# Gate and up projections: the activations' high and low parts in two runs instead of interleaved

## The chip, the cores and the metric

The kernel runs on one core of one Trainium2 chip. The metric is the device time of one execution in microseconds (us), the median of several runs; lower is better.

## What is computed

The reference is one decoder block over 272 positions (16 meta tokens and 256 of the sequence) with model width 2048: a norm, a wide input projection, RWKV-7 time mixing and a forgetting attention side by side, a gated merge, an output projection, and then the feed-forward part, which is where the change lies:

```python
h = h + merged @ w_o
gate, up = jnp.split(_rms(h, n2) @ w_gu, 2, axis=-1)   # w_gu: 2048 x 11264
return h + (jax.nn.silu(gate) * up) @ w_dn             # w_dn: 5632 x 2048
```

Only the 256 positions of the sequence are returned, so the feed-forward part works on 256 positions.

## The kernel before

**Split products.** Every float32 operand is split into a high part (rounded to TensorE's fp32r format) and a low part (the rest). A product is then high times high, high times low and low times high, added up in PSUM. ScalarE makes the high part of a weight tile (`wh`, line 335) and VectorE its low part (`wl`, line 336), each from one 512 KB load `raw` of 128 partitions by 1024 numbers.

**Gate and up.** The loop at line 1385 runs over 11 groups of 512 columns of `w_gate_up`; each group first does gate (tile names `gt`), then up (`up`). `cm_jobs` (line 450) cuts each into 8 jobs (one load of weights each). A job holds two channel tiles `kt` of the contraction (2 of 16; each is 128 channels on the 128 partitions), and runs over 4 blocks of 128 output columns (`m`), and inside over the two channel tiles: so TensorE's order is even `kt`, odd `kt`, even `kt`, odd `kt`, with a new PSUM bank at each even one. For each `m` and `kt`, `mm2` (line 437) issues two matmuls, a **pair**: one of 512 columns (line 441: the weights' high part against the high 256 and the low 256 positions of that channel tile, an access of two pieces of 256), and one of 256 columns (line 443: the weights' low part against the high 256 positions). For the last channel tile (`kt` = 15) the 256-column matmul comes first (line 440). That makes 11 x 2 x 8 x 8 = 1408 pairs, 2816 matmuls. Each matmul has a weight load of its own (128 columns, PEld in the profile), which runs beside the matmul ahead of it.

**The activations.** `hts` holds both parts. In before it is a tile of 16 channel tiles x 2 parts x 272 numbers (L = NMETA + T = 16 + 256; the first 16 of each 272 are not used here). So within a partition the high part of a channel tile begins 64 bytes into its 1088, the low part 1088 bytes further on, and the next channel tile 2176 bytes on. As 2176 is 8 x 256 + 128, the start of an even channel tile and that of an odd one differ by 128 modulo 256, and all even ones are alike modulo 256. The weights' places (`PLACE`, line 59, used at lines 331 to 334) are the same modulo 256 for all four buffers of `wh`, and for all four of `wl`.

**Who writes and reuses hts.** Each of four column groups of the output projection (`wo`, line 1337) ends with transposes, a scaling and a `split` into `hts` (line 1353). After gate and up, the tile's memory is used again for `sst` (line 1414), sums of pairs for the products of the down projection (`dn` and `dnp`).

**Other stages named below.** `zg` (the gate projections of the first half, line 1233) uses `mm2` and `PLACE` as gate and up do, on `xhl`, which is laid out like the old `hts`. `br` (line 1283) uses `mm3` (three matmuls of 256 columns) and the places `APART`, by which the weights of an odd channel tile lie 128 bytes further modulo 256 than those of an even one, as its activations do. `dn` (lines 1460 to 1462) uses three matmuls of 512 columns, with the weights as the moving operand; those alternate by 128 bytes modulo 256 as well.

**What sets the order.** TensorE's instructions stand in the order in which they are written; other engines are scheduled around them. Waits follow from tiles, not from parts of tiles.

Of the kernel before, what the change touches and what calls it, by code (L numbers as in the profile page):

```python
# [10 lines left out]
F32R = mybir.dt.float32r  # L11
# [7 lines left out]
P = 128  # L19
D = 2048  # L20
NMETA = 16

T = 256
L = NMETA + T
# [3 lines left out]
DFF = 5632  # L28
# [6 lines left out]
KT = D // P  # L35
# [23 lines left out]
PLACE = (0, 16, 24)  # L59
APART = (1, 32, 32)  # L60
PLACE_T = (8, 16)

LANES = 108
BETWEEN = 2
# [52 lines left out]
def hybrid_block(ctx, tc, A, out, dbg=None):  # L117
# [18 lines left out]
    def aux_ps(name):  # L136
        return psa.tile([P, 512], F32, tag="aux", name=name)
# [88 lines left out]
    def vc(name, i=0):  # L226
        c = COLS[name] + i
        return vcol[:, c:c + 1]
# [132 lines left out]
    def kblock(ap):  # L361
        return ap.rearrange("(k p) c -> p k c", p=P)

    def mm3(ps, wh, wl, ah, al, first, last):
        nc.tensor.matmul(ps, wh, ah, start=first, stop=False)  # L365
        nc.tensor.matmul(ps, wh, al, start=False, stop=False)  # L366
        nc.tensor.matmul(ps, wl, ah, start=False, stop=last)  # L367
# [29 lines left out]
    def slot(ns):  # L397


        clock[0] += ns  # L400
        if clock[0] < clock[1]:
            return
        due = sorted((st for st in streams if st[0] <= clock[0]), key=lambda st: st[0])
        group = []
        for st in due:
            if st[2] and st[2][0] == "fox":
                mate = [c for c in streams if c[2] and c[2][0] == "chain" and st[2][1] + c[2][1] <= 8 - PSM]
                if mate and mate[0][0] > clock[0] and clock[0] < st[0] + HOLD and mate[0][0] < st[0] + HOLD:
                    continue
                group = [c for c in mate if c[0] <= clock[0]] + [st]  # L410
            else:
                group = [st]
                if st[2]:
                    group += [c for c in due if c[2] and c[2][0] == "fox" and st[2][1] + c[2][1] <= 8 - PSM][:1]
            break
        if group:
            clock[2] = 0.0
            for st in group:
                stage(st)
            clock[1] = clock[0] + max(GAP, MIX * clock[2])  # L420

    def finish_job():
        if pending:
            pending.pop()()

    def run(jobs):
        for load, mul in jobs:
            w = load()
            finish_job()
            pending.append(lambda w=w, mul=mul: mul(w))  # L430
# [6 lines left out]
    def mm2(ps, wh, wl, act, first, last):  # L437

        if last:
            nc.tensor.matmul(ps[:, :T], wl, act[:, 0, :], start=False, stop=False)  # L440
        nc.tensor.matmul(ps.rearrange("p (a t) -> p a t", a=2), wh, act, start=first, stop=last)  # L441
        if not last:
            nc.tensor.matmul(ps[:, :T], wl, act[:, 0, :], start=False, stop=False)  # L443

    def halves(dst, ps):

        nc.scalar.activation(dst, ps[:, :T], AF.Copy)
        nc.vector.tensor_tensor(dst, dst, ps[:, T:], op=ALU.add)

    def cm_jobs(wap, nk, act, n0, n, post, alloc=main_ps, name="cm", two=True, lay=PLACE):  # L450


        box = []
        cols = wap.shape[1]
        nm, kb = cols // P, 1024 // cols

        def mk(q):
            def load():
                return wload([(P, 0, [kb, cols], [((ALL,), kblock(wap[q * kb * P:(q + 1) * kb * P, :]))])], 1024,
                             lay=lay)  # L460

            def mul(w):
                (wh, wl), = w
                if q == 0:
                    box.extend(alloc(f"{name}_{m}") for m in range(nm))
                for m in range(nm):
                    ms = slice(m * P, (m + 1) * P)
                    for k in range(kb):
                        kt = q * kb + k
                        a = act[:, kt, :, n0:n0 + n]  # L470
                        if n == T and two:
                            mm2(box[m], wh[:, k % 2, k // 2, ms], wl[:, k % 2, k // 2, ms], a, kt == 0, kt == nk - 1)
                        else:
                            mm3(box[m][:, :n], wh[:, k % 2, k // 2, ms], wl[:, k % 2, k // 2, ms], a[:, 0], a[:, 1],
                                kt == 0, kt == nk - 1)
                        slot(3 * n / 2.4)
                if q == nk // kb - 1:
                    post(box)
            return load, mul
        return [mk(q) for q in range(nk // kb)]  # L480
# [28 lines left out]
    def split(hi, lo_, src):  # L509
        nc.scalar.activation(hi, src, AF.Copy)  # L510
        nc.vector.tensor_tensor(lo_, src, hi.bitcast(F32), op=ALU.subtract)
# [169 lines left out]
    def rwkv_jobs(g):  # L681
# [14 lines left out]
        for nm, off, full in (("k", 1024, True), ("v", 2048, True), ("r", 0, False)):  # L696
            n0, n = (0, L) if full else (14, T + 2)
            jobs += cm_jobs(w_in[:, off + c0:off + c0 + 256], KT, xhl, n0, n, post(nm, off, full), name=f"{nm}{g}", lay=APART)
# [512 lines left out]
    gt = None  # L1211
# [36 lines left out]
    gt = gt_pool.__enter__()  # L1248
# [52 lines left out]
    hp = hp_pool.__enter__()  # L1301
    hh = hp.tile([P, 2, D], F32, tag="hh", name="hh")

    hts = hp.tile([P, KT, 2, L], F32R, tag="hts", name="hts")
    ss2 = hp.tile([P, 2, 4], F32, tag="ss2", name="ss2")
    rs2 = hp.tile([P, 2], F32, tag="rs2", name="rs2")
    rsb2 = hp.tile([P, T], F32, tag="rsb2", name="rsb2")

    def tm_jobs(wap, nk, ah, al, post, name, lay=PLACE_T):

# [26 lines left out]
    for j in range(4):  # L1337
        js = slice(j * 512, (j + 1) * 512)
        nc.sync.dma_start(hh[:, :, js], x[:, js].rearrange("(t p) c -> p t c", p=P))

        def post(t, ps, j=j, js=js):
            nc.vector.tensor_tensor(hh[:, t, js], ps, hh[:, t, js], op=ALU.add)
            jk = hp.tile([P, 512], F32, tag="jk", name=f"jk{j}{t}", bufs=2)
            nc.scalar.activation(jk, hh[:, t, js], AF.Square, accum_out=ss2[:, t, j:j + 1])
            if t == 0:
                return
            for k in range(4 * j, 4 * j + 4):
                pt = aux_ps(f"hT{k}")[:, :T]
                for t in range(2):
                    nc.tensor.transpose(pt[:, t * P:(t + 1) * P], hh[:, t, k * P:(k + 1) * P], ident)  # L1350
                tmp = hp.tile([P, T], F32, tag="htmp", name=f"htmp{k}", bufs=3)
                nc.vector.tensor_scalar(tmp, pt, vc("n2", k), None, op0=ALU.mult)
                split(hts[:, k, 0, NMETA:], hts[:, k, 1, NMETA:], tmp)
        run(tm_jobs(A["w_o"][0][:, js], KT, mgh, mgl, post, f"wo{j}"))
    finish_job()
    nc.vector.tensor_reduce(rs2, ss2, axis=AX.X, op=ALU.add)
# [27 lines left out]
    wgu = A["w_gate_up"][0]  # L1384
    for j in range(DFF // 512):
        gs = [hp.tile([P, T], F32, tag="ga", name=f"ga{j}{m}", bufs=8) for m in range(4)]

        def post_gate(pss, gs=gs):
            for g, ps in zip(gs, pss):
                halves(g, ps)  # L1390
                nc.vector.tensor_tensor(g, g, rsb2, op=ALU.mult)
                nc.scalar.activation(g, g, AF.Silu)

        def post_up(pss, gs=gs, j=j):
            for m, (g, ps) in enumerate(zip(gs, pss)):
                ub = hp.tile([P, T], F32, tag="ub", name=f"ub{j}{m}", bufs=2)
                halves(ub, ps)
                nc.vector.tensor_tensor(ub, ub, rsb2, op=ALU.mult)
                nc.vector.tensor_tensor(ub, ub, g, op=ALU.mult)
                split(ach[:, 4 * j + m, :], acl[:, 4 * j + m, :], ub)  # L1400
        run(cm_jobs(wgu[:, j * 512:(j + 1) * 512], KT, hts, NMETA, T, post_gate, name=f"gt{j}"))
        run(cm_jobs(wgu[:, DFF + j * 512:DFF + (j + 1) * 512], KT, hts, NMETA, T, post_up, alloc=aux_ps, name=f"up{j}"))

# [5 lines left out]
    fast = FAST  # L1411
    slow = [i for i in range(NF // 2) if i not in fast]
    acp_h, acp_l = (t.rearrange("p (i k) (t c) -> p i k t c", k=2, t=2) for t in (ach, acl))
    sst = hp.tile([P, KT, 2, L], F32R, tag="hts", name="sst").rearrange("p k a t -> p (k a t)")
    sst = sst[:, :len(fast) * 6 * P].rearrange("p (i s a c) -> p i s a c", i=len(fast), s=3, a=2)

    def sums_of_pairs():
# [47 lines left out]
    def split_tiles():  # L1465
        return [wp.tile([P, WCOLS], F32R, tag=t, name=t, bufs=WB).rearrange("p (r c) -> p r c", c=L)[:, :, s:s + T]
                for t, s in zip(("wh", "wl"), PLACE_T)]

    def slow_jobs(i, cg, cs, end):
        def mk(x_):  # L1470
            def load():
                j = 2 * cg + x_
                return wload([(P, 0, [2, 512], [((ALL,), kblock(wdn[i * 256:(i + 1) * 256, j * 512:(j + 1) * 512]))])],
                             1024, lay=(None, *PLACE_T))

# [160 lines left out]
```

## Time and profile before

| | |
|---|---|
| median of 3 runs | 1522.12 us (1520.21, 1522.12, 1522.53) |
| profiled execution, first to last instruction (its span) | 1517.7 us |
| median less span | 4.4 us |
| gate and up, from the first matmul to the last | 788.8 to 1278.1 us |
| TensorE busy share of the span | 99% |

The profile gives no time of the profiled execution other than its span. A row of the trace names the line, the engine, the operation, and the tiles (out<-in). A matmul's shown duration runs past the start of the next one, since matmuls are pipelined: the step from one start to the next is what adds up to time.

### The profile page before, as it was taken

The numbers are of one execution on the slowest core, as the hardware profiler recorded it, in microseconds if no ns is written. First come the engines' busy times: TensorE is split into PE (matmuls) and PEld (weight loads), VectorE is DVE, ScalarE is ACT, GpSimd is POOL, SyncE is SP. The second block draws the span as 40 slices with busy tenths as digits, with TensorE's granted clock in tenths as the row PEclk, the third lists the DMA queues.
The fourth block names the chain that finished last, engine by engine and source line by source line (L and its number), as shares of the span: only waits on it lengthen the run. The fifth ranks groups of instructions, "written<-read, shape, count | busy, mean of one in ns | idle before, by whom it ended". The sixth has DMA issues, their size and how long they took to land.

```text
span 1517.7 us, 26174 instructions
## 1 busy us (share of the span) xinstructions
PE 1509.9 (99%) x10071; PEld 1339.5 (88%) x10071; DVE 1112.0 (73%) x2009; ACT 808.3 (53%) x1230; POOL 99.3 (7%) x182
## 2 busy tenths in 40 slices
PE   9999999999999999999999999999999999999998
PEld 9999999999989888998888888888888888887887
DVE  7888699689789857875665666566566658879776
ACT  7664565475465545644554555454455545554543
POOL 2112202202202000000000000000000000000000
PEclk9999999999999999999999999999999999999999
DMA  8557456646645757777566666666666666566664
GB/s 271 166 166 212 119 156 185 170 122 173 188 127 149 223 152 214 234 231 240 181 179 192 189 187 193 191 186 192 190 187 191 193 186 182 178 211 201 213 206 138
DMA packets 210365, 283.32 MB, mean 187 GB/s; under 512 B 24320, under 2 KB 129296, under 8 KB 210240
## 3 DMA queue, kind: packets, MB, share of 16 engines
q1 hardware_dynamic: 205344, 277.25, 61.9%
q10 hardware_dynamic: 4896, 4.40, 0.9%
q8 instruction: 79, 1.29, 0.3%
q14 instruction: 46, 0.38, 0.1%
HBM read 274.36 MB, written 7.24 MB: 186 GB/s over the span
## 4 chain that ended last, share of the span: by engine, by line
PE 95%; DVE 3%; DMA 1%; issue 1%; ACT 0%; SPq 0%; DVEq 0%; ACTq 0%
PE up L441 11%; PE gt L441 11%; PE zg L441 8%; PE gt L443 5%; PE up L443 5%; PE dn L1461 4%; PE dn L1460 4%; PE dn L1462 4%; PE zg L443 4%; PE f L441 2%; PE br L365 2%; PE br L366 2%; PE br L367 2%; PE f L365 2%; PE wo L1329 2%; PE wo L1331 2%
## 5 line engine op out<-in xcount | busy, mean ns | idle before, releaser
L336 DVE TENSOR_TENSOR wl<-raw,wh 128x1024 fp32r<-128x1024 f32 x460 | 561.9, 1226 | 281.3 <-ACT wh L335 280.6
L335 ACT ACTIVATE wh<-raw 128x1024 fp32r<-128x1024 f32 x460 | 486.5, 1059 | 470.2 <-PE up L441 118.9
L441 PE MATMUL gt<-hts,wh 128*128 128x512 f32 x704 | 242.9, 393 | 0.0
L441 PE MATMUL up<-hts,wh 128*128 128x512 f32 x704 | 242.7, 392 | 0.0
L443 PE MATMUL gt<-hts,wl 128*128 128x256 f32 x660 | 184.8, 280 | 0.0
L443 PE MATMUL up<-hts,wl 128*128 128x256 f32 x660 | 184.6, 280 | 0.0
L441 PE MATMUL zg<-xhl,wh 128*128 128x512 f32 x512 | 181.2, 399 | 0.0
L441 PEld LDWEIGHTS up<-hts,wh 128*128 128x128 f32 x704 | 130.0, 188 | 25.2
L441 PEld LDWEIGHTS gt<-hts,wh 128*128 128x128 f32 x704 | 129.9, 188 | 25.1
L443 PE MATMUL zg<-xhl,wl 128*128 128x256 f32 x480 | 134.3, 280 | 0.0
L443 PEld LDWEIGHTS up<-hts,wl 128*128 128x128 f32 x660 | 125.3, 190 | 1.8
L443 PEld LDWEIGHTS gt<-hts,wl 128*128 128x128 f32 x660 | 125.3, 190 | 1.8
L441 PEld LDWEIGHTS zg<-xhl,wh 128*128 128x128 f32 x512 | 94.3, 188 | 18.7 <-issue 0.7
L1460 PE MATMUL dn<-wh,ach 128*128 128x512 f32 x282 | 110.7, 393 | 0.0
L1461 PE MATMUL dn<-wh,acl 128*128 128x512 f32 x282 | 110.6, 392 | 0.0
L1462 PE MATMUL dn<-wl,ach 128*128 128x512 f32 x282 | 110.5, 393 | 0.0
L443 PEld LDWEIGHTS zg<-xhl,wl 128*128 128x128 f32 x480 | 90.9, 189 | 1.2
L365 PE MATMUL f<-xhl,wh 128*128 128x272 f32 x256 | 75.9, 296 | 0.0
L367 PE MATMUL f<-xhl,wl 128*128 128x272 f32 x256 | 73.6, 288 | 0.0
L366 PE MATMUL f<-xhl,wh 128*128 128x272 f32 x256 | 73.6, 288 | 0.0
L1462 PEld LDWEIGHTS dn<-wl,ach 128*128 128x128 f32 x282 | 52.9, 187 | 12.3 <-DVE wl L336 0.3
L1461 PEld LDWEIGHTS dn<-wh,acl 128*128 128x128 f32 x282 | 52.9, 188 | 12.0
(493 smaller groups left out, 3056.7 us busy)
## 6 DMA issues: line engine op xcount, KB each, us to landing
raw<-in_w_gate_up_dram SPq DMA_DIRECT2D x176, 512.0 KB, 4.3
raw<-in_w_in_dram SPq DMA_DIRECT2D x160, 512.0 KB, 3.9
raw<-in_w_down_dram SPq DMA_DIRECT2D x74, 512.0 KB, 5.0
raw<-in_w_o_dram SPq DMA_DIRECT2D x32, 512.0 KB, 4.3
raw<-in_w_branch_a_dram SPq DMA_DIRECT2D x16, 512.0 KB, 4.6
raw<-in_w_branch_b_dram SPq DMA_DIRECT2D x16, 512.0 KB, 5.0
raw<-in_w_down_dram SPq DMA_DIRECT2D x28, 256.0 KB, 4.6
zgd<-zg ACTq DMA_DIRECT2D x30, 128.0 KB, 3.8
```

The source lines that it names most:

```text
L335: nc.scalar.activation(th, rr, AF.Copy)
L336: nc.vector.tensor_tensor(tl, rr, th.bitcast(F32), op=ALU.subtract)
L365: nc.tensor.matmul(ps, wh, ah, start=first, stop=False)
L366: nc.tensor.matmul(ps, wh, al, start=False, stop=False)
L367: nc.tensor.matmul(ps, wl, ah, start=False, stop=last)
L441: nc.tensor.matmul(ps.rearrange("p (a t) -> p a t", a=2), wh, act, start=first, stop=last)
L443: nc.tensor.matmul(ps[:, :T], wl, act[:, 0, :], start=False, stop=False)
L1329: nc.tensor.matmul(o, ah[:, kt, ts_], hi, start=first, stop=False)
L1331: nc.tensor.matmul(o, ah[:, kt, ts_], lo_, start=False, stop=last)
L1460: nc.tensor.matmul(o, a[0], hi, start=first, stop=False)
L1461: nc.tensor.matmul(o, a[1], hi, start=False, stop=False)
L1462: nc.tensor.matmul(o, a[0], lo_, start=False, stop=last)
```

## The change

`hts` becomes one run of numbers per part: 16 unused numbers, then the high part of all 16 channel tiles one behind the other (16 x 256), then again 16 unused numbers and the low part. `HPART` = 16 x 256 + 16 = 4112 numbers is the distance from a high to its low part (16448 bytes, 64 modulo 256, as 1088 was). A channel tile now follows the one before it at 1024 bytes, so that all 16 start alike modulo 256. The tile shrinks from 34816 to 32896 bytes a partition; its own start is the same byte as before, and what is allocated behind it (`ss2`, `rsb2`, `jk`, `htmp`, `ga`, `ub`, ...) moves down by 1920 bytes. `sst` starts at the same byte. No instruction is added, removed or moved: every engine has the same instructions in the same order, with the same waits; only addresses and one step of an access differ.

```diff
+HPART = KT * T + NMETA
+HTS = 2 * HPART
...
-    hts = hp.tile([P, KT, 2, L], F32R, tag="hts", name="hts")
+    hts = hp.tile([P, HTS], F32R, tag="hts", name="hts")[:, :2 * HPART].rearrange("p (a e) -> p a e", a=2)
+    hts = hts[:, :, NMETA:].rearrange("p a (k t) -> p k a t", t=T)
...
-                split(hts[:, k, 0, NMETA:], hts[:, k, 1, NMETA:], tmp)
+                split(hts[:, k, 0], hts[:, k, 1], tmp)
...
-        run(cm_jobs(wgu[:, j * 512:(j + 1) * 512], KT, hts, NMETA, T, post_gate, name=f"gt{j}"))
-        run(cm_jobs(wgu[:, DFF + j * 512:DFF + (j + 1) * 512], KT, hts, NMETA, T, post_up, alloc=aux_ps, name=f"up{j}"))
+        run(cm_jobs(wgu[:, j * 512:(j + 1) * 512], KT, hts, 0, T, post_gate, name=f"gt{j}"))
+        run(cm_jobs(wgu[:, DFF + j * 512:DFF + (j + 1) * 512], KT, hts, 0, T, post_up, alloc=aux_ps, name=f"up{j}"))
...
-    sst = hp.tile([P, KT, 2, L], F32R, tag="hts", name="sst").rearrange("p k a t -> p (k a t)")
+    sst = hp.tile([P, HTS], F32R, tag="hts", name="sst")
```

## Rows read from the trace of the kernel before

**Rows 1.** The page: busy time, and the granted clock by slices.

```profile
PE 1509.9 (99%) x10071; PEld 1339.5 (88%) x10071; DVE 1112.0 (73%) x2009; ACT 808.3 (53%) x1230; POOL 99.3 (7%) x182
...
PEclk9999999999999999999999999999999999999999
```

**Rows 2.** Busy time by stretches: output projection, gate and up, down projection.

```profile
core 0: us, PE busy (x) PEld busy (x) DVE busy (x) ACT busy (x) POOL busy (x), PEclk, DMA share, GB/s
736.00:789.00 53.00, 53.00 (x239) 42.87 (x238) 31.72 (x40) 24.81 (x35) 0.00 (x0) 1.00 0.61 185
789.00:1278.00 489.00, 489.00 (x2825) 431.45 (x2825) 306.44 (x462) 246.66 (x356) 0.00 (x0) 1.00 0.66 189
1278.00:1517.00 239.00, 235.12 (x1018) 189.96 (x1016) 191.87 (x253) 118.90 (x136) 0.00 (x0) 1.00 0.59 190
```

**Rows 3.** Groups of instructions in 790 to 1277 us; idle time stands last.

```profile
L441 PE MATMUL gt<-hts,wh 128*128 128x512 f32 x702 | 242.2, 393 | 0.0
...
L336 DVE TENSOR_TENSOR wl<-raw,wh 128x1024 fp32r<-128x1024 f32 x176 | 215.5, 1224 | 182.0 <-ACT wh L335 182.0
L335 ACT ACTIVATE wh<-raw 128x1024 fp32r<-128x1024 f32 x175 | 185.8, 1062 | 227.5 <-PE up L441 117.9 <-PE gt L441 105.2 <-PE up L443 2.0
```

**Rows 4.** Tile up, whole trace: durations min/median/max in ns, first and last start.

```profile
L441 PE MATMUL up<-hts,wh x704: 388/393/398, 812.1 to 1278.1; 128*128 128x512 f32 x176
L443 PE MATMUL up<-hts,wl x660: 278/281/283, 812.4 to 1277.9; 128*128 128x256 f32 x165
```

**Rows 5.** TensorE in order of time, five pairs of up: start, duration (us).

```profile
1002.22 0.39 PE L441 MATMUL up<-hts,wh 128*128 128x512 f32 x1
1002.44 0.28 PE L443 MATMUL up<-hts,wl 128*128 128x256 f32 x1
1002.56 0.40 PE L441 MATMUL up<-hts,wh 128*128 128x512 f32 x1
1002.79 0.28 PE L443 MATMUL up<-hts,wl 128*128 128x256 f32 x1
1002.91 0.39 PE L441 MATMUL up<-hts,wh 128*128 128x512 f32 x1
```

**Rows 6.** The same even pair, then the odd one, and the weight loads beside their long matmuls.

```profile
L441 PE MATMUL up<-hts,wh x1: 388/388/388, 1002.2 to 1002.2; 128*128 128x512 f32 x1
L443 PE MATMUL up<-hts,wl x1: 282/282/282, 1002.4 to 1002.4; 128*128 128x256 f32 x1
L441 PE MATMUL up<-hts,wh x1: 397/397/397, 1002.6 to 1002.6; 128*128 128x512 f32 x1
L443 PE MATMUL up<-hts,wl x1: 278/278/278, 1002.8 to 1002.8; 128*128 128x256 f32 x1
...
L443 PEld LDWEIGHTS up<-hts,wl x1: 188/188/188, 1002.2 to 1002.2; 128*128 128x128 f32 x1
...
L443 PEld LDWEIGHTS up<-hts,wl x1: 192/192/192, 1002.6 to 1002.6; 128*128 128x128 f32 x1
```

**Rows 7.** Tile zg, long matmuls of channel tile 13 (odd), then 14 (even).

```profile
L441 PE MATMUL zg<-xhl,wh x1: 392/392/392, 510.4 to 510.4; 128*128 128x512 f32 x1
...
L441 PE MATMUL zg<-xhl,wh x1: 397/397/397, 510.8 to 510.8; 128*128 128x512 f32 x1
```

**Rows 8.** Tile dn, 1292 to 1310 us (one row a line, each third matmul).

```profile
L1461 PE MATMUL dn<-wh,acl x27: 387/388/396, 1291.7 to 1309.6; 128*128 128x512 f32 x27
L1462 PE MATMUL dn<-wl,ach x27: 392/392/393, 1291.9 to 1309.8; 128*128 128x512 f32 x27
```

**Rows 9.** Tile br, TensorE, first and last of six lines with 128 matmuls each.

```profile
L365 PE MATMUL br<-yas,wh x128: 279/280/285, 606.8 to 691.5; 128*128 128x256 f32 x128
...
L367 PE MATMUL br<-ybs,wl x128: 278/281/282, 612.7 to 697.4; 128*128 128x256 f32 x128
```

## The prediction

> **What bounds the kernel now.** I read the page first: TensorE is busy for 99% of the span and its granted clock is full in every slice [rows 1], so time is what TensorE's stream takes, and there is no clock to win back. Then the stretches: gate and up take 489 us, TensorE has no gap in them, VectorE is busy for 306 us of them, ScalarE for 247, the DMA engines for 0.66 [rows 2]. The groups of that stretch say the same from the other side: the matmuls have 0.0 us of idle time before them, while ScalarE's splits of the weights wait 225 us in total for gate and up matmuls to give their tiles back [rows 3]. So the weights come early, TensorE sets the pace, and what the change is worth is the number of matmuls times what each gets shorter or longer. Nothing else can move the end.
>
> **The pace of a pair.** From the first up matmul (812.1 us) to the last (1278.1) are 466.0 us, with the last matmul's own step about 466.2, and they hold 21 groups of 64 pairs [rows 4]: 466.2 / 1344 = 346.9 ns a pair. In order of time the pairs alternate: even channel tile 0.34 us from start to start, odd 0.35 [rows 5]. The durations say it to the ns: even 388 and 282, odd 397 and 278, and the weight load beside the odd long matmul takes 192 ns where that beside the even one takes 188 [rows 6]. A duration is longer than the step to the next start; if by the same amount for all four, it is by (388 + 282 + 397 + 278) / 4 - 346.9 / 2 = 162.8 ns. So an even pair takes 388 + 282 - 325.6 = 344.4 ns and an odd one 349.4. Operation, shapes, engines and weights' residues modulo 256 are the same in both; the activations' start modulo 256 differs by 128. So places in SBUF do show in the time of a matmul here.
>
> **The change, part by part.**
>
> *Nothing is issued more or less, later or earlier.* Instructions, order and waits are unchanged, so there is no term for a new wait, a DMA or a queue.
>
> *The distance of the low part* goes from 1088 to 16448 bytes. Both are 64 modulo 256, the long matmul keeps its access of two pieces of 256 numbers, and I cost it at 0. If only the size of the jump mattered, no row of before prices it; its bounds are those of the whole pair below.
>
> *Tiles behind `hts`* move by 1920 bytes (128 modulo 256). VectorE and ScalarE work on them, with 183 and 242 us of slack in the stretch [rows 2]; these would have to become slower by more than half to be seen. Cost 0. If the slack were gone, TensorE would wait for `wl`, of which there are four buffers.
>
> *The step of 1024 bytes.* This is the term. All channel tiles now start as the even ones did modulo 256, high part and low part, against weights that haven't moved. The price is 1408 pairs times the change of a pair:
> - at the best, each pair has the shorter long matmul and the shorter short one: 388 + 278 - 325.6 = 340.4, or -6.5 ns x 1408 = -9.2 us;
> - all pairs as the even ones: 704 odd pairs lose 5.0 ns, -3.5 us;
> - no change of the mean: 0;
> - all pairs as the odd ones: +2.5 x 1408 = +3.5 us;
> - at the worst, 397 + 282 - 325.6 = 353.4, or +6.5 x 1408 = +9.2 us.
>
> **Why I take 0.** The obvious reading is that the odd pairs' 5 ns are a conflict and go away. Two rows speak against it. In `zg`, which has the same residues, the odd channel tile 13 shows 392 ns and the even tile 14 shows 397 [rows 7]: the long one has changed places, after another run-up (before it stood the reversed order of channel tile 15). So 397 is no property of the even or the odd residue; something is carried from matmul to matmul, and a long one pays for what its predecessors left. And in `dn`, where weights and activations have changed roles and other residues, the matmuls of 512 columns show 387 to 396 ns, yet 26 steps of three take 17.9 us [rows 8]: 17.9 / 78 = 229.5 ns a matmul. In gate and up the mean of the long one is (388 + 397) / 2 - 162.8 = 229.7. Two stages with other places have the same mean and other spreads. I read this as a rate of the matmul with its weight load, around which the starts swing by some ns; places then decide how the time is shared out among neighbours, not how much there is. With a constant residue I expect other, perhaps equal, durations, and about the same 346.9.
>
> The Trainium skill, "SBUF — State Buffer", section "Who interferes with whom", gives TensorE two independent read ports, one for the moving operand and one for weight loads, and says that it waits for nobody. By that rule no address could matter and the change would be worth 0. The 388 against 397 ns, and 188 against 192 for the weight load [rows 6], don't agree with it to the ns, and so I don't rest the sum on it; that the means of two stages agree [rows 4, 8] does go with it.
>
> The sum against the profiled execution: 1517.7 + 0 = 1517.7 us of span. The median of the runs is 4.4 us above that span, so I forecast 1522 us, within 2 us either way if the mean of a pair stays within 1.4 ns.
>
> **The rivals.**
>
> *All pairs as the even ones (faster).* For it: in the steady state of gate and up the even residue is always the shorter pair [rows 5, 6], with the shorter weight load, and the change gives every channel tile just that residue. Against it: rows 7, and that an even matmul so far always came after an odd one; the short 388 may be what follows a long one. Price 704 x 5.0 = 3.5 us: 1518.6 us, and down to 1513 us if the short matmuls fall to 278 as well. It decides for faster once a pair is under 344.8 ns (3.0 us over 1408 pairs).
>
> *A lasting collision (slower).* If the residue at which moving data and weights meet is carried from pair to pair, alternating by 128 bytes may be what breaks it, and a constant one locks every long matmul into the form of 397 ns with a weight load of 192. For it: `br`, where `APART` moves weights and activations together, so that their distance modulo 256 doesn't alternate, takes 697.4 - 606.8 = 90.6 us for 767 steps [rows 9], 118.1 ns, where the matmuls of 256 columns in gate and up take (282 + 278) / 2 - 162.8 = 117.2. By columns that is 0.9 x 3 = 2.7 ns a pair, 3.8 us. Against it: `br` has no matmul of 512 columns and other residues. Price +3.5 us by the odd pairs, +3.8 by `br`: 1525.6 to 1526 us. It decides for slower over 349.0 ns a pair.
>
> **How the numbers follow.** A measurement of this kernel can tell about 0.2% (3 us) from no change. No change of the mean: 0.48, at 1522 us (1520 to 1524). All pairs as the even ones, or better: 0.28, at 1518.6. A lasting collision: 0.24, at 1525.6. So faster 0.28, same 0.48, slower 0.24. The ends at 9.2 us need both matmuls of a pair at their extremes together, which no neighbouring rows show; I leave about 0.1 beyond each end and take 1515.5 to 1527.5.
>
> **What the profile of the changed kernel would show.** Gate and up still without idle time before the matmuls; if there is some, the term is not TensorE's pace and this working is wrong. The alternation in steps of two pairs should be gone or changed, since nothing alternates by channel tile any more; if it is still there, even 388 and odd 397, the residue was never its cause. From the first up matmul to the last 466 us: 463 or less is the faster rival, 469 or more the slower one. Weight loads beside long matmuls at 192 ns throughout show the collision; at 188 throughout with steps of 0.34 us, the even pairs. Output and down projection should stay at 53.0 and 239 us; if they move, the shifted tiles matter, which I cost at nothing.

## The result: slower by 0.17%

| | before | after |
|---|---|---|
| median of 21 runs each | 1520.64 us (1519.54 to 1522.53) | 1523.29 us (1521.76 to 1525.77) |
| profiled execution, span | 1517.7 us | 1520.9 us |
| gate and up, first matmul to last | 788.8 to 1278.1 = 489.3 us | 788.0 to 1279.6 = 491.6 us |

The ratio is 1.0017, with a 95% interval of 1.001 to 1.0023: 1.5 to 3.5 us slower, 2.65 us by the medians. The time lies in the range that I gave, but the case that I took for the likeliest, a pace that stays, did not come about. That 1523.29 us also lies within the 1520 to 1524 us that I gave for that case is luck: I had counted from a median of 1522.12 us over three runs, and over 21 before has 1520.64. One run of before, among those beside the last kernels below, had a granted clock of 0.64 and took 2152.45 us; no figure here includes it.

The page of after first, then the stretches, cut as in [rows 2]; gate and up now last to 1280 us.

```profile
PE 1512.0 (99%) x10071; PEld 1337.6 (88%) x10071; DVE 1111.3 (73%) x2009; ACT 807.7 (53%) x1230; POOL 100.5 (7%) x182
...
PEclk9999999999999999999999999999999999999999
```

```profile
736.00:789.00 53.00, 53.00 (x241) 42.93 (x241) 31.76 (x40) 25.64 (x36) 0.00 (x0) 1.00 0.61 181
789.00:1280.00 491.00, 491.00 (x2821) 430.31 (x2821) 306.39 (x462) 245.83 (x356) 0.00 (x0) 1.00 0.65 189
1280.00:1520.00 240.00, 234.99 (x1015) 189.28 (x1013) 191.50 (x252) 119.12 (x136) 0.00 (x0) 1.00 0.60 189
```

The counts are those of [rows 1], the clock is full, TensorE has no gap in gate and up, and VectorE and ScalarE do the same work in the same time as in [rows 2]. The groups of 790 to 1277 us (as [rows 3]):

```profile
L444 PE MATMUL gt<-hts,wh 128*128 128x512 f32 x701 | 243.0, 394 | 0.0
...
L339 DVE TENSOR_TENSOR wl<-raw,wh 128x1024 fp32r<-128x1024 f32 x175 | 214.2, 1224 | 182.7 <-ACT wh L338 182.7
L338 ACT ACTIVATE wh<-raw 128x1024 fp32r<-128x1024 f32 x174 | 184.5, 1060 | 228.4 <-PE up L444 117.3 <-PE gt L444 106.6 <-PE up L446 2.0
```

There is still 0.0 us before the matmuls, and ScalarE still waits for them, 228 us in place of 227. So in gate and up the same matmuls in the same unbroken stream take longer. Tile `up` over the whole trace, against [rows 4]:

```profile
L444 PE MATMUL up<-hts,wh x704: 390/394/398, 811.4 to 1279.6; 128*128 128x512 f32 x176
L446 PE MATMUL up<-hts,wl x660: 277/279/281, 811.6 to 1279.4; 128*128 128x256 f32 x165
```

From first to last are 468.2 us where before has 466.0. With the last matmul's own 0.23 that is 468.43 / 1344 = **348.5 ns a pair against 346.9**, and 1.6 x 1408 = 2.3 us: the 2.3 us by which gate and up grew, and nearly all of the 2.65. All pace figures below are worked out like this from that row of each kernel (good to 0.1 ns). Of what is left, 0.3 us, nothing can be said: the interval of the medians is 2 us wide.

The two profiled executions differ in two more places. The earlier stages ended 0.8 us sooner in after. Behind gate and up, after took 1.7 us more; most of that is waits of TensorE for the splits of weights in the down projection, before first, then after:

```profile
PE dnp L1460 <- ACT wh L510: 0.5, 1, 0.5
PE dnp L1462 <- DVE wl L511: 0.2, 1, 0.2
```

```profile
PE dnp L1466 <- DVE wl L514: 1.6, 3, 0.8
PE dnp L1464 <- ACT wh L513: 0.5, 1, 0.5
```

(The numbers are us in total, times, and the longest.) These waits come and go without the change: before_w_alt below, on the layout of before, has 2.4 us in place of the 0.2.

In order of time (start, duration in us), five pairs as in [rows 5], and the next that stands eight pairs after the first:

```profile
1002.06 0.40 PE L444 MATMUL up<-hts,wh 128*128 128x512 f32 x1
1002.30 0.28 PE L446 MATMUL up<-hts,wl 128*128 128x256 f32 x1
1002.41 0.39 PE L444 MATMUL up<-hts,wh 128*128 128x512 f32 x1
1002.64 0.28 PE L446 MATMUL up<-hts,wl 128*128 128x256 f32 x1
1002.76 0.40 PE L444 MATMUL up<-hts,wh 128*128 128x512 f32 x1
1003.00 0.28 PE L446 MATMUL up<-hts,wl 128*128 128x256 f32 x1
1003.11 0.39 PE L444 MATMUL up<-hts,wh 128*128 128x512 f32 x1
1003.35 0.28 PE L446 MATMUL up<-hts,wl 128*128 128x256 f32 x1
1003.46 0.39 PE L444 MATMUL up<-hts,wh 128*128 128x512 f32 x1
...
1004.85 0.40 PE L444 MATMUL up<-hts,wh 128*128 128x512 f32 x1
```

The 0.34, 0.35, 0.34, 0.35 of before is gone; these four steps are all 0.35 (rounded), and the pattern repeats after eight pairs (one load of weights) instead of two. The weight loads of the same tile, 1000 to 1003.5 us, and the one among them that takes longest:

```profile
L446 PEld LDWEIGHTS up<-hts,wl x11: 188/189/192, 1000.0 to 1003.5; 128*128 128x128 f32 x11
...
L446 PEld LDWEIGHTS up<-hts,wl x1: 192/192/192, 1001.7 to 1001.7; 128*128 128x128 f32 x1
```

The long form of 192 ns, in [rows 6] beside each odd pair, has become rarer: the median is 189, and over the whole of `up` 77 of 704 loads of `wl` take 192 ns, where in before 308 do.

### The profile page after: what moved, and what is told of

It is laid out like the page before. It is cut to its first block, busy times and chain, and to the rows that moved or that the text cites. A ratio compares the mean times of both kernels' runs of the same rounds, so it can differ in the third digit from the quotient of the medians.

```text
span 1520.9 us, 26174 instructions
## 1 busy us (share of the span) xinstructions
PE 1512.0 (99%) x10071; PEld 1337.6 (88%) x10071; DVE 1111.3 (73%) x2009; ACT 807.7 (53%) x1230; POOL 100.5 (7%) x182
## 4 chain that ended last, share of the span: by engine, by line
PE 94%; DVE 3%; DMA 1%; issue 1%; ACT 0%; SPq 0%; DVEq 0%; ACTq 0%
PE gt L444 11%; PE up L444 11%; PE zg L444 8%; PE gt L446 5%; PE up L446 5%; PE zg L446 4%; PE dn L1465 3%; PE dn L1464 3%; PE dn L1466 3%; PE f L444 2%; PE br L368 2%; PE br L369 2%; PE br L370 2%; PE f L368 2%; PE wo L1333 2%; PE wo L1335 2%
```

## The experiments

The question is which part of the change slows TensorE: the low part lying far away, the tiles behind `hts` having moved, or the channel tiles all starting alike modulo 256; and if it is the last, by what rule. I call three rules R, A and P. **R**: the pace follows from how the moving data lies to the weights that are loaded beside it, and is good as long as that alternates. **A**: each such distance has a price of its own, which adds up over the matmuls. **P**: the operands' own starts modulo 256 count, each by itself.

Distances are given as (long, short): the start of the moving data less the start of the weights loaded beside that matmul, modulo 256, worked out from where the program puts the tiles. Before alternates between (224, 0) and (96, 128) from channel tile to channel tile; after has (224, 0) throughout. `lay` sets the weights' places: whether those of odd channel tiles lie 128 bytes further, and the first number of `wh` and of `wl` (4 bytes each; `PLACE` is (0, 16, 24)). "64 pairs" is the time of one gate or up from its first matmul's start to the next one's, in the trace. The texts put on record ahead of the runs give paces about 0.2 ns lower (346.7 for before, 348.3 for the changed kernel), and two of them give 346.7 for lo_0 as well, where 22.233 us / 64 is 347.4; by 64 pairs all can be compared. One time a kernel, beside one of before on the same chip, except for the last three, which have 15 of before beside them (median 1520.86 us).

| kernel | distances (long, short) | first to last up, us | a pair, ns | 64 pairs, us | time (before beside it), us |
|---|---|---|---|---|---|
| before | (224, 0) / (96, 128) | 466.0 | 346.9 | 22.200 | |
| after | (224, 0) | 468.2 | 348.5 | 22.307 | |
| alt_two_runs | (224, 0) / (96, 128) | 466.0 | 346.9 | 22.200 | 1520.73 (1521.0) |
| const_near | (224, 0) | 468.2 | 348.5 | 22.307 | 1522.04 (1521.0) |
| before_w_alt | (224, 128), weights and activations alternate | 469.8 | 349.7 | 22.387 | 1526.2 (1521.0) |
| after_w_alt | (224, 128) / (96, 0), weights alternate alone | 470.2 | 350.0 | 22.400 | 1525.17 (1521.0) |
| all_odd | (96, 128) | 474.1 | 352.9 | 22.587 | 1528.78 (1520.34) |
| wh_128 | (224, 128) | 465.7 | 346.7 | 22.187 | 1520.05 (1520.34) |
| wl_128 | (96, 0) | 470.2 | 350.0 | 22.400 | 1525.5 (1520.34) |
| lo_0 | (224, 0), low part 64 less | 466.7 | 347.4 | 22.233 | 1520.94 (1520.34) |
| shift_64_all | (224, 0), all 64 further | 468.2 | 348.5 | 22.307 | 1524.92 (1520.29) |
| before_wh_128 | (224, 128) / (96, 0) | 469.1 | 349.2 | 22.347 | 1524.23 (1520.29) |
| one_piece | as lo_0, one access of 512 | 466.7 | 347.4 | 22.233 | 1521.9 (1520.29) |
| wh_128_lo_0 | (224, 128), low part 64 less | 471.9 | 351.3 | 22.480 | 1529.43 (1520.29) |
| wh_64 | (224, 192) | 470.6 | 350.3 | 22.420 | 1524.53 (1520.86) |
| wl_64 | (160, 0) | 470.4 | 350.2 | 22.413 | 1524.14 (1520.86) |
| wh_128_timed | (224, 128) | 465.7 | 346.7 | 22.187 | below |

### Which part of the change

**alt_two_runs** keeps the two runs, a far low part (16704 bytes, 64 modulo 256) and moved tiles (by 1408 bytes, 128 modulo 256 as the 1920 of the change), but puts the odd channel tiles behind the even ones, 128 bytes further modulo 256:

```diff
-HPART = KT * T + NMETA
+HPART = KT * T + NMETA + 64
...
+        o = NMETA + k // 2 * T + k % 2 * (KT // 2 * T + 32)
+        return htile[:, :, o:o + T]
```

> The changed kernel with its two runs kept, but within a run the even channel tiles stand first and the odd ones behind them, 128 bytes further modulo 256; the low part is 16704 bytes (64 modulo 256) behind the high one. So the residues alternate by channel tile as in the kernel before, at the distance of the changed one. Measure: start to start of 64 pairs of gate or up (22.200 us before, 22.307 us changed). Theory R (the alternation of residues modulo 256 sets the pace): 22.20 us, and the alternation of 388 and 397 ns is back. Theory D (the far low part sets it): 22.31 us. Theory S (the shifted tiles behind hts): 22.31 us, as they are shifted here too.

Its tile `up`, and four of its long matmuls among the rest in order of time:

```profile
L453 PE MATMUL up<-hts,wh x704: 388/393/398, 811.3 to 1277.3; 128*128 128x512 f32 x176
```

```profile
1000.03 0.39 PE L453 MATMUL up<-hts,wh 128*128 128x512 f32 x1
...
1000.38 0.40 PE L453 MATMUL up<-hts,wh 128*128 128x512 f32 x1
...
1000.73 0.39 PE L453 MATMUL up<-hts,wh 128*128 128x512 f32 x1
...
1001.07 0.40 PE L453 MATMUL up<-hts,wh 128*128 128x512 f32 x1
```

466.0 us from first to last, as before, with the durations of [rows 4] (388 to 398, median 393) and the alternation of [rows 5] back. So neither the two runs nor the low part's distance beyond its residue nor the moved tiles cost gate and up anything that can be seen.

**const_near** is the opposite: the parts lie near each other again, in groups of two channel tiles, and all tiles start alike modulo 256.

```diff
-HTS = 2 * HPART
+HTS = KT * 2 * L
...
+        o = NMETA + k % 2 * T
+        return htile[:, k // 2, :1056].rearrange("p (a e) -> p a e", a=2)[:, :, o:o + T]
```

> High and low parts interleaved in groups of two channel tiles, low part 2112 bytes behind the high one (64 modulo 256), groups 4352 bytes apart: all channel tiles start alike modulo 256 as in the changed kernel, but the parts lie near each other, and the tile has the size of before, so that nothing behind it is shifted. Theory R: 22.31 us for 64 pairs and the eight-pair pattern of the changed kernel. Theory D and theory S: 22.20 us.

```profile
L453 PE MATMUL up<-hts,wh x704: 390/394/398, 811.6 to 1279.8; 128*128 128x512 f32 x176
```

468.2 us, and after's durations (390, 394, 398). With these two the part is settled: the loss of pace is the constant residue, all of it, with the weights at the places that they have in before.

### By what rule

**before_w_alt and after_w_alt** let the weights of odd channel tiles lie 128 bytes further, on the layout of before and of after: `lay=(1, 16, 24)` for both loops, no other edit.

```diff
-post_gate, name=f"gt{j}"))
+post_gate, name=f"gt{j}", lay=(1, 16, 24)))
...
-post_up, alloc=aux_ps, name=f"up{j}"))
+post_up, alloc=aux_ps, name=f"up{j}", lay=(1, 16, 24)))
```

> The kernel before with hts as it was (residues alternate by 128 bytes), but the weights of the odd channel tiles of gate and up also 128 bytes further modulo 256, so that activations and weights keep their distance modulo 256 and both alternate. Theory R as a relation (what counts is the distance modulo 256 between the moving data and the weights being loaded): 22.31 us as in the changed kernel. Theory R as the activations' own residue (the step from one matmul's moving data to the next one's): 22.20 us as in the kernel before.

> The changed kernel (activations' residue constant) with the weights of the odd channel tiles of gate and up 128 bytes further modulo 256: the distance between moving data and weights alternates by 128 again. Theory R as a relation: 22.20 us and the alternation of 388 and 397 ns, as in the kernel before. Theory R as the activations' own residue: 22.31 us, as in the changed kernel.

```profile
L441 PE MATMUL up<-hts,wh x704: 392/392/400, 811.7 to 1281.5; 128*128 128x512 f32 x176
```

```profile
L444 PE MATMUL up<-hts,wh x704: 392/394/399, 812.2 to 1282.4; 128*128 128x512 f32 x176
```

Both (before_w_alt first) are slower than before and after, 349.7 and 350.0 ns. R as I had put it falls: after_w_alt has the alternation of distances that it asks for, and is the worse for it. Part of that is a mistake of mine: the weights loaded beside a short matmul are those of the next channel tile, so that alternating weights give other distances at the short matmul than alternating activations do, (224, 128) and (96, 0) for after_w_alt in place of before's (224, 0) and (96, 128).

**all_odd, wh_128, wl_128** hold one distance throughout: after's runs 128 bytes further; the weights' high part 128 bytes further; their low part 128 bytes further.

```diff
-HTS = 2 * HPART
+HTS = 2 * HPART + 32
...
-name="hts")[:, :2 * HPART]
+name="hts")[:, 32:]
```

For wh_128 `lay=(0, 48, 24)`, for wl_128 `lay=(0, 16, 56)`.

> The changed kernel with its two runs 128 bytes further on, so that every channel tile starts as the odd ones did before. Call a pair by two distances modulo 256: moving data minus the weights loaded beside it, for the long matmul and for the short one. Before: 224 and 0 for even, 96 and 128 for odd, 346.7 ns on average; changed: 224 and 0 for all, 348.3; this one: 96 and 128 for all. Theory A (each pair has a price by its two distances, and prices add up): 2 x 346.7 - 348.3 = 345.0 ns, 64 pairs in 22.09 us. Theory K (a constant pattern always keeps a collision alive): 348.3 ns or more, 22.31 us or more.

> The changed kernel with the high parts of gate and up weights 128 bytes further on, all of them: distances 224 and 128 for every pair. The kernel of before with alternating weights had the same two distances at alternating places and took 350.0 ns a pair. Theory A: 350.0 ns here too, 22.40 us for 64 pairs, with its pattern of two pairs. If the own places or the steps from one matmul's place to the next matter besides the distances: another number.

> The changed kernel with the low parts of gate and up weights 128 bytes further on: distances 96 and 0 for every pair. The changed kernel with alternating weights mixed 224 and 128 with 96 and 0 and took 350.0 ns on average. Theory A: 2 x 350.0 - 350.0 = 350.0 ns, 22.40 us for 64 pairs. Theory K: 348.3 or more.

all_odd, its tile `up`, and two pairs in order of time:

```profile
L444 PE MATMUL up<-hts,wh x704: 387/395/396, 812.0 to 1286.1; 128*128 128x512 f32 x176
```

```profile
1000.08 0.40 PE L444 MATMUL up<-hts,wh 128*128 128x512 f32 x1
1000.31 0.28 PE L446 MATMUL up<-hts,wl 128*128 128x256 f32 x1
1000.43 0.40 PE L444 MATMUL up<-hts,wh 128*128 128x512 f32 x1
1000.66 0.28 PE L446 MATMUL up<-hts,wl 128*128 128x256 f32 x1
1000.78 0.40 PE L444 MATMUL up<-hts,wh 128*128 128x512 f32 x1
```

Nearly every pair is the same here, at 0.35 us, and first to last takes 474.1 us: the odd residue by itself costs 352.9 ns, the even one (after) 348.5, and alternating between the two (before) 346.9, less than either. wh_128:

```profile
L444 PE MATMUL up<-hts,wh x704: 392/393/399, 811.6 to 1277.3; 128*128 128x512 f32 x176
```

465.7 us: one shift of the weights' high part by 128 bytes gives back what the change lost. A falls with these four: if distances had prices that add up, (224, 0) and (96, 128) would cost together what (224, 128) and (96, 0) cost, but 348.5 + 352.9 = 701.4 ns and 346.7 + 350.0 = 696.7. (The 350.0 of wl_128 is what A had given for it; its 345.0 for all_odd and 350.0 for wh_128 were not met.) Theory K falls with wh_128: a constant pattern needn't be slow. And wh_128 and before_w_alt have (224, 128) at every pair alike, and take 346.7 and 349.7 ns: the distances beside each matmul do not fix the pace.

The edits of `lay` also move what ScalarE and VectorE write. Read from the starts in the traces, that isn't what costs time: in all_odd the pairs that run (for nine tenths of their time or more) during one of ScalarE's splits of weights average 353.3 ns, and so do those that run beside none (a tenth of their time at most); in wh_128 both average 346.7. For VectorE's splits it is 353.3 and 353.4, and 346.6 and 346.7.

**lo_0** takes the 16 unused numbers out between the runs, so that a low part lies 16384 bytes behind its high part, 0 modulo 256 instead of 64. **one_piece** has the same residues, but each low part directly behind its high part, so that the long matmul reads one piece of 512 numbers:

```diff
-HPART = KT * T + NMETA
-HTS = 2 * HPART
+HPART = KT * T
+HTS = 2 * HPART + NMETA
```

```diff
+    hts = hp.tile([P, HTS], F32R, tag="hts", name="hts")[:, NMETA:].rearrange("p (k a t) -> p k a t", a=2, t=T)
```

> The changed kernel with the low run 16384 bytes behind the high one (0 modulo 256) instead of 16448 (64). Distances of the starts stay 224 and 0. If only the data that move while the weights are being loaded count, and these are the high part's, nothing changes: 348.3 ns, 22.31 us. If the low part's place counts too: another number, between 345 and 350 ns by the values seen so far.

> The low part of a channel tile directly behind its high part (1024 bytes), channel tiles 2048 bytes apart, all alike modulo 256: the long matmul reads one piece of 512 numbers in place of two of 256, at the residues of the run with the low part at 0. If the break between two pieces costs anything of its own: under 346.7 ns a pair, up to some 7 ns less (the 16 cycles by which the long matmul is above the short one), 22.2 us down to 21.8. Theory Q: 346.7 ns, 22.23 us, as in that run.

```profile
L444 PE MATMUL up<-hts,wh x704: 389/394/403, 811.9 to 1278.6; 128*128 128x512 f32 x176
```

```profile
L444 PE MATMUL up<-hts,wh x704: 389/394/403, 811.5 to 1278.2; 128*128 128x512 f32 x176
```

Both (lo_0 first): 466.7 us, 347.4 ns, the same durations. So the low part's residue counts too (348.5 to 347.4), and the break between the two pieces of the access costs nothing at these residues.

**shift_64_all** moves activations and both parts of the weights by 64 bytes together (`[:, 16:]` for the activations, `lay=(0, 32, 40)`).

> The changed kernel with the activations' runs and both parts of gate and up weights moved by 64 bytes together: every distance between moving data and weights stays as in the changed kernel, every own place modulo 256 is another. Theory Q (a pair has a floor of 346.7 ns, and what comes on top is decided by distances modulo 256 among the data read, not by the places themselves): 348.3 ns and the same eight-pair pattern, 22.307 us for 64 pairs. Theory P (own places modulo 256 count): another number.

```profile
L444 PE MATMUL up<-hts,wh x704: 390/394/398, 812.3 to 1280.5; 128*128 128x512 f32 x176
```

468.2 us with after's durations. P falls: a shift of all three by 64 bytes changes nothing, so what matters here are places against each other. (Its run was 1524.92 us all told; gate and up account for none of what it has over after.)

**before_wh_128** is before with `lay=(0, 48, 24)`; it alternates between the two distances that after_w_alt alternates between. **wh_128_lo_0** joins two edits that each helped.

> The kernel before with the high parts of gate and up weights 128 bytes further on: distances 224 and 128 for even channel tiles, 96 and 0 for odd ones. The changed kernel with alternating weights had just this sequence of distances between moving data and weights, and took 350.0 ns a pair; only the steps from one matmul's activations to the next one's differ (128 modulo 256 here, 0 there). If the distances between moving data and weights are all that counts: 350.0 ns, 22.40 us. If the steps among the activations count as well: another number, 346.7 or more by theory Q.

> The changed kernel with both of the edits that alone gave 346.7 ns: high parts of the weights 128 bytes further on, and the low run at 0 modulo 256. Theory Q: no pair below the floor, 346.7 ns or more, 22.19 us or more for 64 pairs. If each edit takes 1.7 ns off whatever the other does: 345.0 ns, 22.08 us.

```profile
L441 PE MATMUL up<-hts,wh x704: 388/392/399, 811.9 to 1281.0; 128*128 128x512 f32 x176
```

before_wh_128 took 349.2 ns, after_w_alt 350.0 (22.347 and 22.400 us for 64 pairs): the same distances to the weights, not the same pace, so these distances in their order don't fix it either. What differs between the two is how the activations lie to one another, and how the weights do; which of these has the share wasn't separated. wh_128_lo_0, tile `up`:

```profile
L444 PE MATMUL up<-hts,wh x704: 389/394/408, 813.5 to 1285.4; 128*128 128x512 f32 x176
```

351.3 ns, from two edits that alone gave 346.7 and 347.4: what the edits are worth doesn't add up.

### A version without the loss, and two more places

**wh_128_timed** is wh_128 again, with more runs; **wh_64** (`lay=(0, 32, 24)`) and **wl_64** (`lay=(0, 16, 40)`) look for a pace under 346.7 at distances between.

> The changed kernel with the high parts of gate and up weights 128 bytes further on, timed. By its pace (22.187 us for 64 pairs, against 22.200 before and 22.307 changed) 22 x 0.013 = 0.3 us under the kernel before, which its measurement can't tell from it, and 2.6 us under the changed kernel: ratio to before 0.9995 to 1.000. If the loss of the changed kernel lies elsewhere than in the pace of the pairs: 1.0015 or more.

> The changed kernel with the high parts of gate and up weights 64 bytes further on: distances 224 and 192. Theory Q (a floor): 346.7 ns a pair or more, 22.19 us or more for 64 pairs. Theory V (346.7 is no floor): a value under it.

> The changed kernel with the low parts of gate and up weights 64 bytes further on: distances 160 and 0. Theory Q: 346.7 ns a pair or more, 22.19 us or more. Theory V: a value under it.

wh_128_timed: 1520.14 us median of 11 runs, ratio to before 0.9996, interval 0.9987 to 1.0005; its row repeats to 0.1 us (811.8 to 1277.5). The two runs of memory with the weights 128 bytes further cost what before costs; that they are better can't be told. As its tiles lie where after's do, and only the places of its weights differ, this also bears out that after's loss is the pace. wh_64 and wl_64 took 350.3 and 350.2 ns, slower than after.

## Why the prediction was wrong

**What held.** The bound: in gate and up TensorE's stream has no gap and no waits in either kernel, and what they lost is pace. The jump to the low part and the tiles behind `hts`: 0 in gate and up, as costed, by alt_two_runs, whose jump and shift have other sizes but the same residues, and by wh_128_timed, which has the very 16448 and 1920 bytes and before's time. The alternation of two pairs is gone, as the residue's doing. The output projection takes what it took: its last matmul starts 91.1 us behind its first in both (697.5 to 788.6, 696.6 to 787.7; the 53.0 us of [rows 2] are only the part of it in that window).

"Nothing else can move the end" did not hold to the size of this change: behind the last up matmul the 17 traces take 239.6 to 242.9 us to their ends, for the most part by what TensorE waits in the down projection.

**The step that failed** is "Why I take 0": that a matmul with its weight load has a rate of its own, around which starts swing, and that places only share the time out among neighbours. The places set the rate. Moving nothing but operands, gate and up ran at 346.7, 346.9, 347.4, 348.5, 349.2, 349.7, 350.0, 350.3, 351.3 and 352.9 ns a pair: 1.8% from end to end, 465.7 to 474.1 us in the stretch. What the rate theory had seen may be a floor: of 16 layouts none ran below before's pace by more than 0.2 ns, and two others reach it. If it is one, before stood on it, so that, as far as these layouts tell, the change could only keep the pace or lose; I had no row that said so, and gave 0.28 to a gain.

The 0 entered the sum without a row in which the activations' residue is constant, and it measured +2.3 us (1.6 ns x 1408).

My two rows for it were weaker than I took them to be. [rows 7] did show that 397 ns is no property of a residue, and the sequel bears that out: in lo_0 all pairs have the same residues, and yet (by the starts in the trace) they take 352.9 and 340.5 ns in turn. But "something is carried from matmul to matmul" says only that neighbours count, not that their sum is fixed. [rows 8] compared two stages that both alternate by 128 bytes; equal means there say nothing about a stage that doesn't alternate. The account of the kernel ahead says of `dn` that it alternates; I didn't use it.

**The other numbers of the sum.** The bounds of the term were -9.2 to +9.2 us. The one on the slow side is near what the slowest layout did, 352.9 ns in all_odd against 353.4, but by luck: its matmuls show 395 and 281 ns, for which my sum, with 325.6 ns taken off, gives 350.4. So the amount by which durations run past the next start isn't the same in every layout. The 4.4 us between the span and the median were too large a term as well: in after's 21 runs a time is 1.7 to 2.2 us above its own span, and the rest was the scatter of the runs.

**The faster rival** (all pairs as the even ones) fails as I had argued against it: the short 388 of an even pair in [rows 6] does not stay when no odd pair stands ahead. With the even residue alone the long matmuls take 390 to 398 and the pair 348.5 ns, not 344.4 (by the starts in the trace, before's even pairs take 343.5 ns and its odd ones 350.0). The two states of an alternation aren't to be had one by one: each residue alone is slower than both in turn.

**The slower rival** (a lasting collision) was right in its sign and in that alternating is what kept the pace, for this layout of the weights, and wrong in its form and its price. I had each long matmul at 397 ns beside a weight load of 192, +3.5 us; after has that form only now and then, and +2.3; its 468.2 us from the first up matmul to the last stand between the 466 and the 469 that I had named. And all_odd, the slowest of all, shows what that form is worth as a mark: its weight loads beside the long matmuls stand at 187 to 188 ns from end to end:

```profile
L446 PEld LDWEIGHTS up<-hts,wl x660: 187/188/188, 812.0 to 1285.6; 128*128 128x128 f32 x165
```

So a weight load of 192 ns is not what a slow pace is made of. `br`, from which I had taken +3.8 us, would have been the better neighbour of the two stages that I used, with a distance that doesn't alternate; that it was slow for this reason was not tried.

**The rule cited ahead.** By the Trainium skill, "SBUF — State Buffer", section "Who interferes with whom", moving data and weight loads have independent ports and TensorE waits for nobody. The traces show no wait of a matmul in gate and up, but at the same instructions and the same clock the pace depends on where the operands lie, 346.7 to 352.9 ns; the measurement decides, and the rule can't be used to cost a layout at 0.

**What stays open.** Why a place costs 1.6, 3 or 6 ns a pair. That two reads of TensorE collide is the reading that suggests itself, but no run shows a collision. The modulus of 256 bytes fits the runs: const_near's groups of two channel tiles lie 4352 = 17 x 256 bytes apart and after's tiles 1024, and both take 22.307 us for 64 pairs, while 128 bytes make a difference (before against after). Moves that aren't multiples of 64 bytes weren't tried. The three rules tried (R, A, P) are refuted as single rules. What is shown is that places count relative to each other and in sequence: distance to the weights beside (wh_128, wl_128), residue of the low part (lo_0), what alternates (before_wh_128 against after_w_alt). A rule that gives all these paces I don't have. As for the rest of the kernel, the time after the last up matmul is 241.3 us in after (1520.9 - 1279.6) and 239.6 in before (1517.7 - 1278.1), but 240.5 in const_near (1520.3 - 1279.8) with before's size of `hts`, and 242.9 in before_w_alt (1524.4 - 1281.5), where nothing behind it was shifted. So no cost of the moved tiles shows in it; why the splits come late there in one execution and not in another wasn't pursued.

## What to carry to other kernels

When TensorE's stream has no gaps, a change of operand addresses need not be free: read its pace over a long block of equal matmuls (first start, last start, count) before and after, which here repeats to 0.1 us in 466 us where single runs scatter by 3. When a trace alternates between a shorter and a longer form, don't price a kernel that has the shorter form alone; it is the sequence that has a pace, and here both residues alone were slower. And when the step between tiles changes its residue, try the weights at other places with it: here one constant in `lay` took the loss away, while the four others that were tried alone on the same layout (after_w_alt, wl_128, wh_64, wl_64) made it larger.

## What the runs showed of the hardware

- At full clock and with no wait shown, the pace of a pair of fp32r matmuls (512 and 256 columns, each with its weight load) went from 346.7 to 352.9 ns by the addresses of its operands in SBUF alone.
- Moving activations and weights by 64 bytes together changed nothing to the ns (22.307 us for 64 pairs, both); moving only one of them by 64 or 128 bytes cost up to 4.4 ns a pair or gave back 1.8.
- At the same residues, an access of 512 numbers in two pieces was as fast as one of a single piece (466.7 us, both).
